# High and low activations as one 512-column operand, summed at the read, and the down products bank by bank, in a float32 transformer stack on one core

## The chip, the cores and the metric

One core of one Trainium2 chip runs the whole kernel. The metric is device time in microseconds, the median of three runs. The engines are named as in the profile: PE is TensorE's matmul stream and PEld its weight loads, DVE is VectorE, ACT is ScalarE, POOL is GpSimd, SP is SyncE, which issues the weights' DMA.

## What is computed

The input is 256 rows of tokens with 1024 features. Five layers follow, all in float32: four of a first block and one of a second.

```python
# first block: layer i has a mixer of kind i % 3 and a feed-forward part
h = layer_norm(ALPHA * h + mix, ln_g[i, 0], ln_b[i, 0])      # retention, rglru, mla, retention
h = layer_norm(ALPHA * h + sq_relu_mlp(h, mlp_w1[i], mlp_w2[i]), ln_g[i, 1], ln_b[i, 1])

def sq_relu_mlp(x, w1, w2):                                   # 1024 -> 4096 -> 1024
    return jnp.square(jax.nn.relu(x @ w1)) @ w2

# second block
x = x + 0.5 * swiglu(rmsnorm(x, ffn1_norm), ffn1_w1, ffn1_w3, ffn1_w2)   # 1024 -> 2816 -> 1024
x = x + hybrid_mixer(rmsnorm(x, mix_norm), ...)               # two attentions with gates
x = x + 0.5 * swiglu(rmsnorm(x, ffn2_norm), ffn2_w1, ffn2_w3, ffn2_w2)
return rmsnorm(x, final_norm)

def swiglu(x, w1, w3, w2):
    return (jax.nn.silu(x @ w1) * (x @ w3)) @ w2
```

## The kernel before

**Split operands.** TensorE takes a float32 operand in one pass only with fewer bits, so each operand is split into a high part (a ScalarE copy to float32r) and a low part (a VectorE subtraction). A product is then three matmuls: high by high, high by low, low by high. `split` does this for activations, `pump` for weights: it issues the DMA of a weight chunk on SyncE up to 8 chunks ahead, and the chunk's cast on ScalarE (line 368, `hl<-raw`) and its low part on VectorE up to 5 chunks ahead. `get` fetches the next chunk and calls `pump`. The transposed activations of a layer are `xT[:, k, a, tok]`: k is one of 8 blocks of 128 features, a is high or low, tok one of 256 tokens, so that `xT[:, k]` is 512 contiguous columns.

**Products.** All matmuls are issued by the helper `mm` at line 315. `ws` holds weights stationary: for each k it issues three matmuls of 256 columns (weights high by x high, weights high by x low, weights low by x high), all into the same 256 columns of a PSUM bank. `xs` holds the activations stationary. `down` is the second product of a feed-forward layer, and the output product of a mixer: hidden values `a` (high) and `b` (low) of one token tile are stationary, and 512 columns of weights move; the six matmuls alternate between the two banks of the tile's accumulators. `down_tail` issues the last chunks of a layer bank by bank. `front` makes the first six chunks of a layer; the two parts of x already go into separate columns there and are summed by `front_sum` when the bank is read: a ScalarE copy to `tmp` (line 549) and a VectorE add.

**PSUM.** Eight banks: four accumulators (`accp`) and a common pool of four (`pp`, taken by `psb`). `front` takes two accumulators and four banks of the pool, the tiles `fr`.

**Order.** The order on every engine is the order of the program text; each engine works its own queue in that order and waits for others by semaphores. In `mlp` a step j makes one chunk of hidden values (two steps share a bank, and the second one reads it: ReLU, square and split on ScalarE and VectorE), and 8 steps later `down` consumes it. `ffn` is alike with two chunks a step and a lag of 5. The recurrent layer `lru` follows the list `LRU_STEPS` from its fourth entry on: "R0 G0 R1 G1 V0 V1 g1 R2 g0 V2 C0 S0 D0 C1 F0 R3 V3 C2 S1 D1 W0 F1 S2 R4 V4 C3 D2 G2 S3 D3 g2 F2 G4 C4 S4 D4 g4 W1 G3 g3 F3 F4 W2 W3 W4". R and G are products with `ws` (two chunks into one bank); V is the convolution on R's bank, first step on ScalarE and six steps on VectorE (`uc`); `gelu_a` reads G's bank with a square on ScalarE and then VectorE; C is the gates' products and ScalarE work, S a square root on ScalarE, D the VectorE chain (`b_`, then `u`) with the scan, F the gated states (`hh`), W the output product. In `mix` the list `MIX_STEPS` does the same for two attentions; it has "Sb0 R1 Nb0 q00 q01 q02 k00 X1 Tb0", where q00 to k00 are products with `ws`, X1 transposes of queries (line 1371) and R1, Nb0 norms on VectorE.

The change touches `ws` (not its body; a sibling is added), `down`, `front_sum`, `mlp`, `ret` (`rope`, `qk`), `lru`, `ffn`, and in `mix` the products of heads of group A (`aproj_qk`) and the gates. In `mla` and in mix's branch products `ws` stays.

Of the kernel before, what the change touches and what calls it, by code (L numbers as in the profile page):

```python
# [9 lines left out]
F32 = mybir.dt.float32  # L10
# [8 lines left out]
P = 128  # L19
S = 256  # L20
# [16 lines left out]
FRONT = 6  # products of a layer that start on the first tile alone  # L37
# chunks at a layer's end that finish the first tile ahead
# [5 lines left out]
MIX_B = (0, 2, 1)  # queries of four heads, keys and values, the other queries  # L44
# R, G, W: products; V: convolution; C, S, D: gates and scan; g: second half of gelu;
# F: the gated states, split
LRU_STEPS = ("R0 G0 R1 G1 V0 V1 g1 R2 g0 V2 C0 S0 D0 C1 F0 R3 V3 C2 S1 D1 W0 F1 S2 R4 "
             "V4 C3 D2 G2 S3 D3 g2 F2 G4 C4 S4 D4 g4 W1 G3 g3 F3 F4 W2 W3 W4").split()
# k, v: keys and values of four heads; q, r, p: queries of two; S, N, T, V: a head's scores,
# norm, transposes and values; o: first rows of the output product  # L50
# [3 lines left out]
# h, j: last chunk of the keys and values, chunks of the last queries of group B; I, R, X:  # L54
# their squares, norm and rope, transposes. q, k, v: projections of a pair of heads of
# group A; S, N, T, V: a head's scores, norm, transposes and values (a: pair, head, tile
# of rows); g: gates; A, B: the branches' products
# [16 lines left out]
def _stream():  # L74
    """Every weight chunk in the order of use: (segment, input, layer, first row,
    row blocks, columns as (start, width) runs)."""
# [126 lines left out]
# chunks that the tensor engine takes whole, as float32  # L203
# [8 lines left out]
# per-partition vectors: name -> (first column, columns)  # L212
# [20 lines left out]
def _consts():  # L233
    """Tables that depend on shapes alone."""
# [47 lines left out]
def kernel(ctx, tc, d, out, dbg=None):  # L282
# [39 lines left out]
    def split(src, h, l):  # L322
        """h + l = src, each of a width that one pass of the tensor engine carries."""
        ns.copy(out=h, in_=src)  # L324
        tt(l, src, h.bitcast(F32), SUB)

# [50 lines left out]
    def low_next(n):  # L377
        """Make the next few of the low parts held back."""
        for _, low in (st["late"] or ())[:n]:
            tt(*low)  # L380
        if st["late"]:
            st["late"] = st["late"][n:]

    def low_parts(late, soon=0):
        """Hold back the low parts of the chunks that come after the next few, or make
        those held back."""
# [8 lines left out]
    def pin(on):  # L395
        """While on, chunks stay until it is off again."""
        st["pin"] = on
        if on:
            st["base"] = st["i"]
# [16 lines left out]
    def ws(ps, ch, xT, kk, c0=0, first=True, last=True):  # L416
        """ps[f, tok] += W[:, c0 + f] . x[tok]; weights stationary."""
# [6 lines left out]

    def xs(ps, ch, xT, t, k0, kk, first, last, w0=0, w=None):
        """ps[tok, n] += x[tok] . W[:, n]; activations stationary."""
# [8 lines left out]
    def xs_front(items, xT, after=None):  # L435
        """Products with stationary activations that begin on the first tile and the
        weights' high parts: yields when the second tile's activations are needed.
        items: name, first block of rows, their number, outs, and if it is the last into
        these; outs[t]: banks, and their columns in the chunk."""
# [21 lines left out]
        if after:  # the first tile ahead  # L461
            order = [(c, t) for t in range(2) for c in range(n)]
# [13 lines left out]
    def down(acc, t, hid, ch, first, last, perm=False):  # L476
        """acc[t][tok, :] += hid[:, tok] . W rows of one block."""
# [6 lines left out]
        for o, w in halves:  # L484
            mm(o, a, l[:, 0, w], False, False)
        for o, w in halves:
            mm(o, b, h[:, 0, w], False, last)

    def down_tail(acc, get_item, n_items, perm=False):
        """The last chunks: the first tile whole, then the second, with two stops before  # L490
        its end. Low parts of the next layer's weights wait till its start."""
# [20 lines left out]
    def front(names, xT, banks, done, stops=(2, 4)):  # L512
        """Products with stationary weights that begin on the first tile alone: yields
        when the second tile's activations are needed. done(n, ps) gets each bank,
        [second][x high, x low][tok], to be summed over the middle."""
# [29 lines left out]
    def front_sum(ps, tmp, o):  # L545
        """o[f, tok] from a bank of front."""
        v = ps.rearrange("p (t a n) -> p t a n", t=2, a=2)
        t3 = tmp.rearrange("p (t n) -> p t n", t=2)
        ns.copy(out=t3, in_=v[:, :, 1])
        tt(o.rearrange("p (t n) -> p t n", t=2), v[:, :, 0], t3, ADD)  # L550

    def front_banks():
        """The first tile's accumulators, then four banks of the common pool."""
# [39 lines left out]
    def rsqrt(o, v, mul, add):  # L593
        """o = (v * mul + add) ** -0.5 for a few columns."""
# [6 lines left out]
    def to_xT(xT, y, t, halves=(0, 1)):  # L601
        for g in halves:
            if t == 0:
                ps = psb("trp")
            else:  # the tile's accumulators are free by then
# [79 lines left out]
    def angles(k):  # L685
        """sin and cos of position times frequency, reduced to within pi of zero."""
# [29 lines left out]
    def gate_tables():  # L716
        # 2 softplus(-lam), and halves of the gate biases
# [30 lines left out]
    def early(j):  # L748
        """Tables of later layers, made in the first layers."""
# [997 lines left out]
```

## Time and profile before

| | |
|---|---|
| median of three runs | 2050.29 us (2049.59 to 2050.74) |
| span of the profiled execution | 2048.1 us |
| PE busy | 2015.0 us, 98% |
| PEld busy | 1814.8 us, 89% |
| DVE busy | 1288.9 us, 63% |
| ACT busy | 1022.5 us, 50% |
| DMA from HBM over the span | 177 GB/s |

The busy time of an engine is the union of its instructions' spans, and matmuls overlap: one of 256 columns is shown with 284 ns from start to end, while the next starts long before. A run of n matmuls that is busy for B and whose matmuls are shown with a latency of L therefore has a rate of (B - L) / (n - 1). In a timeline a row is a run of equal instructions: its start, how long the run was busy, the operation, output and inputs by the program's names, the form of output and input, the count, and in brackets the idle time of the engine before the run and what ended it.

### The profile page before, as it was taken

To read this page: it belongs to the slowest core of one execution; us is meant where nothing else is said; L and a number is where in the kernel's file an instruction comes from. 1 tells how busy PE (TensorE), PEld (TensorE's weight loads), DVE (VectorE), ACT (ScalarE), POOL (GpSimd) and SP (SyncE) were. 2 spreads that over 40 slices of the span, in tenths; PEclk is the share of its full clock that TensorE was granted. 3 is DMA by queue.
4 is the path that set the end of the run, shared out by engine and by line. 5 is a ranking of instruction groups with operands and counts; after the bars stand their busy time and mean duration, and the time that the engine had idled before them with its cause. 6 is when DMAs were issued, how large, how long until landed. Compare 5 with 4: busy or idle time off the path is not lost.

```text
span 2048.1 us, 31960 instructions
## 1 busy us (share of the span) xinstructions
PE 2015.0 (98%) x12814; PEld 1814.8 (89%) x12814; DVE 1288.9 (63%) x1823; ACT 1022.5 (50%) x1493; POOL 72.3 (4%) x114
## 2 busy tenths in 40 slices
PE   8999999999999999999999999999999999999998
PEld 6888989887998889998888899989997999999997
DVE  6667765589645667545766764576557755467554
ACT  5444565485645355554444365544445545445443
POOL 0000000000000100000000100000001100000000
PEclk9999999999999999999999999999999999999999
DMA  8554555464665444654655475546554555365552
GB/s 298 183 174 144 185 197 185 146 209 147 231 199 171 145 133 163 215 188 144 224 176 170 143 279 191 186 144 213 188 176 167 158 139 148 123 201 181 197 186 76
DMA packets 102724, 364.73 MB, mean 178 GB/s; under 512 B 11855, under 2 KB 12527, under 8 KB 102576
## 3 DMA queue, kind: packets, MB, share of 16 engines
q1 hardware_dynamic: 97200, 345.09, 50.3%
q0 software_dynamic: 5376, 17.61, 3.4%
q8 instruction: 100, 1.64, 0.3%
q14 instruction: 48, 0.39, 0.1%
HBM read 360.52 MB, written 2.13 MB: 177 GB/s over the span
## 4 chain that ended last, share of the span: by engine, by line
PE 93%; DVE 4%; ACT 1%; issue 1%; POOL 1%; DMA 0%; SPq 0%; POOLq 0%; ACTq 0%; DVEq 0%
PE pp L315 54%; PE a L315 32%; PE fr L315 4%; DVE x L300 1%; PE ao L315 1%; POOL rs L303 1%; DVE bs L628 1%; DMA raw<-in_w_ret_dram 0%; PE a L609 0%; PE a L1492 0%; ACT hl L368 0%; DVE xT L303 0%; DVE hl L303 0%; PE trp L897 0%; DVE bq L303 0%
## 5 line engine op out<-in xcount | busy, mean ns | idle before, releaser
L303 DVE TENSOR_TENSOR hl<-raw,hl 128x1024 fp32r<-128x1024 f32 (+3 forms) x659 | 765.5, 1200 | 179.9 <-ACT hl L368 179.0
L315 PEld LDWEIGHTS pp<-xT,hl 128*128 128x128 f32 x6384 | 786.8, 192 | 14.4 <-issue 1.6
L315 PE MATMUL pp<-xT,hl 128*128 128x256 f32 x6384 | 798.7, 284 | 0.0
L368 ACT CAST hl<-raw 128x1024 fp32r<-128x1024 f32 (+3 forms) x659 | 650.5, 1031 | 187.7 <-PE a L315 75.7
L315 PE MATMUL a<-hl,h 128*128 128x512 f32 x2064 | 501.8, 394 | 0.0
L315 PEld LDWEIGHTS a<-hl,h 128*128 128x128 f32 x2064 | 381.9, 190 | 75.2
L315 PE MATMUL pp<-hl,xT 128*128 128x512 f32 (+2 forms) x1200 | 269.9, 381 | 2.7 <-ACT hl L368 1.6
L315 PEld LDWEIGHTS pp<-hl,xT 128*128 128x128 f32 x1200 | 219.6, 189 | 40.6 <-DVE xT L303 2.1
L303 DVE TENSOR_TENSOR h<-r,h 128x512 fp32r<-128x512 f32 (+1 forms) x108 | 63.1, 584 | 262.6 <-ACT h L324 262.5
L312 ACT ACTIVATE r<-pp 128x512 f32<-128x512 f32 (+1 forms) x90 | 45.5, 506 | 311.6 <-PE pp L315 311.6
L315 PE MATMUL a<-hl,yT 128*128 128x512 f32 x432 | 104.0, 397 | 0.0
L315 PEld LDWEIGHTS a<-hl,yT 128*128 128x128 f32 x432 | 80.8, 188 | 18.7 <-issue 0.5
L303 POOL TENSOR_TENSOR rs<-ve,mhalf 128x1 f32<-128x1 f32 (+2 forms) x48 | 34.9, 728 | 1745.3 <-DVE ve L306 1741.7
L315 PE MATMUL fr<-xT,hl 128*128 128x256 f32 x672 | 88.4, 285 | 0.0
L324 ACT CAST h<-r 128x512 fp32r<-128x512 f32 (+1 forms) x108 | 57.6, 533 | 57.3 <-DVE r L303 55.2
L315 PEld LDWEIGHTS fr<-xT,hl 128*128 128x128 f32 x672 | 83.4, 192 | 0.0
L300 DVE SCALAR_TENSOR_TENSOR r<-r,pp 128x256 f32<-128x256 f32 x38 | 16.0, 420 | 81.6 <-ACT r L312 81.6
L315 PE MATMUL a<-xT,hl 128*128 128x256 f32 x336 | 45.7, 286 | 4.0 <-DVE xT L303 4.0
L315 PEld LDWEIGHTS a<-xT,hl 128*128 128x128 f32 x336 | 42.1, 191 | 7.5 <-DVE xT L303 7.5
L300 DVE SCALAR_TENSOR_TENSOR x<-x,a 128x512 f32<-128x512 f32 x32 | 21.9, 684 | 32.9 <-PE a L315 32.8
L312 ACT ACTIVATE r<-r 128x512 f32<-128x512 f32 x64 | 40.5, 633 | 2.0
L324 ACT CAST xT<-a 128x512 fp32r<-128x512 f32 x22 | 12.8, 586 | 42.5 <-PE a L609 42.5
(352 smaller groups left out, 1315.1 us busy)
## 6 DMA issues: line engine op xcount, KB each, us to landing
raw<-in_w_mlp_dram SPq DMA_DIRECT2D x256, 512.0 KB, 4.6
raw<-in_w_ffn_dram SPq DMA_DIRECT2D x132, 512.0 KB, 4.5
raw<-in_w_ret_dram SPq DMA_DIRECT2D x128, 512.0 KB, 4.4
raw<-in_w_mix_dram SPq DMA_DIRECT2D x68, 512.0 KB, 4.2
raw<-in_w_lru_dram SPq DMA_DIRECT2D x30, 512.0 KB, 4.7
raw<-in_w_mla_dram SPq DMA_DIRECT2D x12, 512.0 KB, 3.8
raw<-in_w_mix_dram SPq DMA_DIRECT2D x16, 384.0 KB, 3.5
gB<-in_ln_g_dram POOLq DMA_DIRECT2D x8, 512.0 KB, 4.9
```

The lines of the kernel that those rows point to most:

```text
L300: nv.scalar_tensor_tensor(out=o, in0=a, scalar=s, in1=b, op0=op0, op1=op1)
L303: (eng or nv).tensor_tensor(out=o, in0=a, in1=b, op=op)
L312: ns.activation(out=o, in_=i, func=f, **kw)
L315: nt.matmul(out=o, lhsT=a, rhs=b, start=start, stop=stop)
L324: ns.copy(out=h, in_=src)
L368: ns.copy(out=hl[:, 0, :c], in_=t[:, :c])
L628: nv.bn_stats(out=bs[:, n], in_=z[:, w])
```

## The change

A second helper `ws2` is used where `ws` had been with `xT` moving. It issues, for each k, one matmul of 512 columns (weights high by both parts of x, side by side in a whole bank) and one of 256 (weights low by x high, onto the first half). `ws2_sum` adds the halves when the bank is read, with a ScalarE copy and a VectorE add into an SBUF tile, and what read the PSUM bank before reads that tile. Every chunk now takes a bank of its own. `front_sum` copies to its output directly, without `tmp`. `down` issues its six matmuls bank by bank. In `lru` the tag `gs` gets two buffers. The rest of the diff takes comments away and renames ffn's argument.

```diff
+    def ws2(bank, ch, xT, kk, c0=0):
+        h, l = ch
+        w = slice(c0, c0 + P)
+        for k in range(kk):
+            mm(bank, h[:, k, w], xT[:, k], k == 0, False)
+            mm(bank[:, :S], l[:, k, w], xT[:, k, 0, :], False, k == kk - 1)
+
+    def ws2_sum(bank, o):
+        ns.copy(out=o, in_=bank[:, S:])
+        tt(o, bank[:, :S], o, ADD)
...
     def down(acc, t, hid, ch, first, last, perm=False):
...
         for o, w in halves:
             mm(o, a, h[:, 0, w], first, False)
-        for o, w in halves:
             mm(o, a, l[:, 0, w], False, False)
-        for o, w in halves:
             mm(o, b, h[:, 0, w], False, last)
...
-    def front_sum(ps, tmp, o):
+    def front_sum(ps, o):
         v = ps.rearrange("p (t a n) -> p t a n", t=2, a=2)
-        t3 = tmp.rearrange("p (t n) -> p t n", t=2)
-        ns.copy(out=t3, in_=v[:, :, 1])
-        tt(o.rearrange("p (t n) -> p t n", t=2), v[:, :, 0], t3, ADD)
+        o = o.rearrange("p (t n) -> p t n", t=2)
+        ns.copy(out=o, in_=v[:, :, 1])
+        tt(o, v[:, :, 0], o, ADD)
...
                 if j < nf:
                     ch = get("mlp_w1")
+                    ps = psb()
+                    ws2(ps, ch, xT, KD)
                     if j % 2 == 0:
-                        ps = psb().rearrange("p (c n) -> p c n", c=2)
-                    ws(ps[:, j % 2], ch, xT, KD)
+                        su = mp.tile([P, 2, S], F32, tag="su", name="su", bufs=2)
+                    ws2_sum(ps, su[:, j % 2])
                     if j % 2 == 1:
-                        evac(j, ps)
+                        evac(j, su)
...
             def qk(h, nm, mid=None):
-                ps = psb()
+                a = rp.tile([P, 512], F32, tag="ra", name="ra", bufs=1)
+                a = a.rearrange("p (c n) -> p c n", c=2)
                 for c in range(2):
-                    ws(ps[:, c * S:(c + 1) * S], get("ret_w_in"), xT, KD)
+                    ps = psb()
+                    ws2(ps, get("ret_w_in"), xT, KD)
+                    ws2_sum(ps, a[:, c])
                     if c == 0 and mid:
                         mid()
-                hd[h, nm] = rope(ps, nm)
+                hd[h, nm] = rope(a, nm)
...
                 if step in "RG":
-                    ps = psb().rearrange("p (c n) -> p c n", c=2)
+                    tag = "gs" if step == "G" else "xc"
+                    su = lp.tile([P, 2, S], F32, tag=tag, name=tag)
                     for c in range(2):
-                        ws(ps[:, c], get("lru_w_in"), xT, KD)
+                        ps = psb()
+                        ws2(ps, get("lru_w_in"), xT, KD)
+                        ws2_sum(ps, su[:, c])
                     if step == "G":
-                        gelu_a(j, ps)
+                        gelu_a(j, su)
                     else:
-                        xcs[j] = ps
+                        xcs[j] = su
...
                 if j < nf:
-                    ps = psb().rearrange("p (c n) -> p c n", c=2)
-                    ws(ps[:, 0], get(w[0]), xT, KD)
-                    ws(ps[:, 1], get(w[1]), xT, KD)
-                    evac(j, ps[:, 0], ps[:, 1])
+                    su = mp.tile([P, 2, S], F32, tag="su", name="su", bufs=2)
+                    for n in range(2):
+                        ps = psb()
+                        ws2(ps, get(w[n]), xT, KD)
+                        ws2_sum(ps, su[:, n])
+                    evac(j, su[:, 0], su[:, 1])
...
                 ps = psb()
-                ws(ps[:, :S], get("w_in_2"), xT, KD)
-                if c == 0:  # queries of a tile in falling order, as the bias has them
+                ws2(ps, get("w_in_2"), xT, KD)
+                if c == 0:
                     o = qk[:, c, g].rearrange("p (t n) -> p t n", t=2)[:, :, ::-1]
-                    act(o, ps[:, :S].rearrange("p (t n) -> p t n", t=2), AF.Copy, scale=0.125)
+                    v = ps.rearrange("p (a t n) -> p a t n", a=2, t=2)
+                    act(o, v[:, 1], AF.Copy, scale=0.125)
+                    stt(o, v[:, 0], 0.125, o, MUL, ADD)
                 else:
-                    ns.copy(out=qk[:, c, g], in_=ps[:, :S])
+                    ns.copy(out=qk[:, c, g], in_=ps[:, S:])
+                    tt(qk[:, c, g], ps[:, :S], qk[:, c, g], ADD)
...
-                    ws(ps["g"][:, b], get("w_in_2"), xT, KD)
-                    for c in range(2 * b):
-                        act(th[:, 8 * c + n], ps["g"][:, c], AF.Tanh, scale=0.5,
-                            bias=hbg[:, 8 * c + n:8 * c + n + 1])
+                    pg = psb()
+                    ws2(pg, get("w_in_2"), xT, KD)
+                    o = th[:, 8 * b + n]
+                    ws2_sum(pg, o)
+                    act(o, o, AF.Tanh, scale=0.5, bias=hbg[:, 8 * b + n:8 * b + n + 1])
```

## Rows read from the trace of the kernel before

**Rows 1.** Page, part 1: busy time, share of span, instructions.

```profile
PE 2015.0 (98%) x12814; PEld 1814.8 (89%) x12814; DVE 1288.9 (63%) x1823; ACT 1022.5 (50%) x1493; POOL 72.3 (4%) x114
```

**Rows 2.** Timeline of PE, a steady stretch of mlp 0 (columns as told above).

```profile
301.59 3.04 PE L315 MATMUL pp<-xT,hl 128*128 128x256 f32 x24
304.46 2.94 PE L315 MATMUL a<-hl,h 128*128 128x512 f32 x12
307.24 3.04 PE L315 MATMUL pp<-xT,hl 128*128 128x256 f32 x24
```

**Rows 3.** Groups by form, PE: count, busy us, mean ns, idle before.

```profile
L315 PE MATMUL pp<-xT,hl 128*128 128x256 f32 x6384 | 798.7, 284 | 0.0
L315 PE MATMUL pp<-hl,xT 128*128 128x512 f32 x912 | 216.5, 395 | 2.4 <-ACT hl L368 1.6 <-DVE hl L303 0.5 <-DVE xT L303 0.3
```

**Rows 4.** Timeline of PE: values in ret 0; end of mlp 0.

```profile
76.77 11.08 PE L315 MATMUL pp<-hl,xT 128*128 128x512 f32 x48
372.22 23.86 PE L315 MATMUL a<-hl,h 128*128 128x512 f32 x102
```

**Rows 5.** Groups by form, ACT and DVE: the front's sum at the read.

```profile
L549 ACT COPY tmp<-fr 128x256 f32<-128x256 f32 x28 | 9.6, 367 | 0.0
L303 DVE TENSOR_TENSOR su<-fr,tmp 128x256 f32<-128x256 f32 x24 | 9.5, 418 | 0.0
```

**Rows 6.** Timelines of PE and DVE behind the front of mlp 0.

```profile
231.69 8.80 PE L315 MATMUL pp<-xT,hl 128*128 128x256 f32 x72
...
234.53 0.42 DVE L303 TENSOR_TENSOR su<-fr,tmp 128x256 f32<-128x256 f32 x1
...
239.06 0.75 DVE L303 TENSOR_TENSOR su<-fr,tmp 128x256 f32<-128x256 f32 x2
```

**Rows 7.** Timelines of PE and DVE behind the front of ffn 1.

```profile
1372.13 12.04 PE L315 MATMUL pp<-xT,hl 128*128 128x256 f32 x99
...
1375.28 0.42 DVE L303 TENSOR_TENSOR su<-fr,tmp 128x256 f32<-128x256 f32 x1
...
1379.06 0.75 DVE L303 TENSOR_TENSOR su<-fr,tmp 128x256 f32<-128x256 f32 x2
```

**Rows 8.** Timelines of ACT and DVE in lru; last, DVE's group u<-u,e there.

```profile
429.04 1.02 ACT L312 ACTIVATE uc<-pp,vec 128x256 f32<-128x256 f32 x2 [0.26 <-PE pp L315]
443.43 1.01 ACT L312 ACTIVATE uc<-pp,vec 128x256 f32<-128x256 f32 x2
454.28 1.02 ACT L312 ACTIVATE uc<-pp,vec 128x256 f32<-128x256 f32 x2 [1.43 <-PE pp L315]
461.76 0.60 ACT L312 ACTIVATE g<-pp 128x512 f32<-128x512 f32 x1
467.52 0.60 ACT L312 ACTIVATE g<-pp 128x512 f32<-128x512 f32 x1 [0.19 <-PE pp L315]
474.01 0.63 ACT L312 ACTIVATE s__4484<-u 128x512 f32<-128x512 f32 x1
...
432.11 0.69 DVE L300 SCALAR_TENSOR_TENSOR g<-g,gs 128x512 f32<-128x512 f32 x1
444.89 1.26 DVE L300 SCALAR_TENSOR_TENSOR uc<-pp,vec,uc 128x255 f32<-128x255 f32 x3
457.63 2.42 DVE L300 SCALAR_TENSOR_TENSOR uc<-pp,vec,uc 128x255 f32<-128x255 f32 x6
465.99 0.68 DVE L300 SCALAR_TENSOR_TENSOR g<-g,pp 128x512 f32<-128x512 f32 x1
473.93 0.68 DVE L300 SCALAR_TENSOR_TENSOR g<-g,pp 128x512 f32<-128x512 f32 x1
...
L300 DVE SCALAR_TENSOR_TENSOR u<-u,e 128x512 f32<-128x512 f32 x5 | 3.4, 689 | 3.0 <-ACT s__4208 L312 2.6 <-ACT s__4093 L312 0.5
```

**Rows 9.** Timelines of PE and DVE at the start of attention in mix.

```profile
1593.63 1.03 PE L1371 MATMUL trp<-cs,bq 128*128 128x128 f32 x8
...
1593.89 3.82 DVE L303 TENSOR_TENSOR hl<-raw,hl 128x1024 fp32r<-128x1024 f32 x4
```

More of the change, by code (lines that the diff above doesn't have):

```diff
@@ L776, in done @@
                     sums[0] = mp.tile([P, 2, S], F32, tag="su", name="su", bufs=2)
-                tmp = mp.tile([P, S], F32, tag="tmp", name="tmp", bufs=2)
-                front_sum(ps, tmp, sums[0][:, j % 2])
+                front_sum(ps, sums[0][:, j % 2])
                 if j % 2 == 1:
@@ L803, in ret, with rope @@
             hd = {}
-            def rope(ps, nm):
+            def rope(a, nm):
                 cos, sin = trig["cosr"], trig["sinr"]
-                a = rp.tile([P, 512], F32, tag="ra", name="ra", bufs=1)
-                a = a.rearrange("p (c n) -> p c n", c=2)
                 b = rp.tile([P, 2, S], F32, tag="rb", name="rb", bufs=1)
                 o = rp.tile([P, 2, S], F32, tag=nm, name=nm)
-                v = ps.rearrange("p (c n) -> p c n", c=2)
-                tt(a, v, cos[:, None, :].to_broadcast([P, 2, S]), MUL)
-                tt(b, v, sin[:, None, :].to_broadcast([P, 2, S]), MUL)
+                tt(b, a, sin[:, None, :].to_broadcast([P, 2, S]), MUL)
+                tt(a, a, cos[:, None, :].to_broadcast([P, 2, S]), MUL)
                 tt(o[:, 0], a[:, 0], b[:, 1], SUB)
@@ L1023, in finish @@
                 yTs[j] = yT
-            gs = lp.tile([P, 2, S], F32, tag="gs", name="gs", bufs=1)
+            gs = lp.tile([P, 2, S], F32, tag="gs", name="gs")
             def done(n, ps):
@@ L1030, in done @@
                     xcs[j // 2] = lp.tile([P, 2, S], F32, tag="xc", name="xc")
-                tmp = lp.tile([P, S], F32, tag="tmp", name="tmp")
-                front_sum(ps, tmp, gs[:, c] if j == 1 else xcs[j // 2][:, c])
+                front_sum(ps, gs[:, c] if j == 1 else xcs[j // 2][:, c])
                 if c == j == 1:
@@ L1235, in mla, with ffn @@
             yield from down_tail(acc, lambda c: (oT[:, 4 + c], get("mla_w_o")), 4)
-    def ffn(n, xT):
+    def ffn(seg, xT):
         nf = DFF2 // P
         lag = FFN_LAG
-        w = [f"ffn{n}_w{k}_2" for k in (1, 3, 2)]
-        tail = TAIL["ffn", n]
+        w = [f"ffn{seg}_w{k}_2" for k in (1, 3, 2)]
+        tail = TAIL["ffn", seg]
         with tc.tile_pool(name="ffnp", bufs=8) as mp:
@@ L1258, in done @@
                     sums[0] = mp.tile([P, 2, S], F32, tag="su", name="su", bufs=2)
-                tmp = mp.tile([P, S], F32, tag="tmp", name="tmp", bufs=2)
-                front_sum(ps, tmp, sums[0][:, n % 2])
+                front_sum(ps, sums[0][:, n % 2])
                 if n % 2 == 1:
@@ L1264, in ffn @@
             yield from front([w[k % 2] for k in range(FRONT)], xT, front_banks(), done,
-                             (4, 5) if n == 1 else (3, 4))
+                             (4, 5) if seg == 1 else (3, 4))
             acc = acc_new()
@@ L1550, in mix @@
                     b = k[0]
-                    if b == 0:
-                        ps["g"] = psb().rearrange("p (c n) -> p c n", c=2)
-                    ws(ps["g"][:, b], get("w_in_2"), xT, KD)
-                    for c in range(2 * b):
-                        act(th[:, 8 * c + n], ps["g"][:, c], AF.Tanh, scale=0.5,
-                            bias=hbg[:, 8 * c + n:8 * c + n + 1])
+                    pg = psb()
[3 more added lines that the diff above has]
+                    act(o, o, AF.Tanh, scale=0.5, bias=hbg[:, 8 * b + n:8 * b + n + 1])
                 else:
```

## Prediction

> **What bounds the kernel now.** I read the busy line of the page first. TensorE is busy 98% of the span, VectorE 63%, ScalarE 50% [rows 1], so time is made where TensorE's stream gets shorter or where it is made to wait. The second view is the timeline of TensorE in a steady stretch of a feed-forward layer: 24 matmuls of 256 columns, 12 of 512, again 24, with no idle time noted between them, 5.65 us a round [rows 2]. There everything else is hidden. The third view is the timeline of the other two engines in the stretches where they are not hidden: right behind a layer's front, in the middle of the recurrent layer (lru), and at the start of attention in mix. What matters in them is not the busy share but which engine runs behind which, because the change makes ScalarE wait for VectorE in places where today it does not.
>
> The profiled span is 2048.1 us, 2.2 below the median 2050.3; I carry the sum over to the median unchanged.
>
> **The change part by part.**
>
> *One 512-column matmul for two of 256.* In `ws` a step of eight rows of weights issues three matmuls of 256 columns; `ws2` issues one of 512 and one of 256. The columns are the same 768, one matmul and one weight load go. The group that `ws` makes has 6384 matmuls [rows 3], so 2128 steps; by the loops these are 832 in the four mlp, 608 in the two ffn, 256 in the two ret, 320 in mix and 112 in lru, and all of them go over to `ws2`. What is one matmul worth? A run's rate is its busy time less one matmul's latency, over the count less one. 72 matmuls of 256 take 8.80 us [rows 6] with a latency of 0.284 [rows 3], so 119.9 ns each; columns alone at the full 2.4 GHz are 106.7, and 13 ns come on top. For 512 columns the kernel has two rates. Where the transposed activations `xT` are one operand and the split weights `hl` the other, 48 take 11.08 us [rows 4] with a latency of 0.395 [rows 3]: 227.4 ns. Where hidden values are stationary, 102 take 23.86 us: 232.4 ns [rows 4]. The new matmul has the operands of the first row, only with their roles swapped, so I take 227.4. A step then goes from 3 x 119.9 = 359.7 to 227.4 + 119.9 = 347.3: 12.4 ns saved, times 2128 = 26.4 us. The ends: with 232.4 it is 7.4 ns (15.7 us); and the round of [rows 2], 5.65 us, is 16 ns less than 24 x 119.9 + 12 x 232.4 = 5.666, so a change of width may itself give some 8 ns, which would make 20 ns (43 us).
>
> The Trainium skill speaks against this part: TensorE: Matmul & The Clock Gate, section "Back-to-back issue gap", has a fixed cost of only 2.5 ns per matmul beside the columns at 2.4 GHz. The rows above show 13 to 14 ns, so I go by them; by the page's figure the part would be worth 2128 x 2.5 = 5.3 us.
>
> *`down` by bank.* The same twelve matmuls of a pair of tiles in another order. The 102 matmuls in [rows 4] hold both orders: 60 come from `down`, which alternates banks today, and 42 from `down_tail`, which already goes bank by bank. The whole run is at 232.4. I take nothing. Ends: 0, and if it brought 2136 matmuls to 227.4, a gain of 10.7 us. Nothing waits for a bank of `down` alone, since its last flag is never set.
>
> *The sum at the read.* Each of the 266 products of `ws2` adds a ScalarE copy of 256 columns (367 ns) and a VectorE add (418 ns) [rows 5]; two adds in a row take 0.75 [rows 6], so each adds some 0.34 to a full queue. Over the span that is 266 x 0.37 = 98 us of ScalarE and about 90 to 111 us of VectorE, in engines that are idle 1025 and 759 us. In the steady stretch it is free. But both engines work their queues in order, so what counts is where these two stand and who waits behind them. Three places.
>
> *(a) Behind a front.* The front's last four chunks hold all four banks of the common pool. Today two chunks share a bank; now each takes one, so the third chunk behind the front needs the bank of the front's fifth. In mlp 0 the products start at 231.69 [rows 6]. VectorE reads the front's fourth chunk at 234.53 to 234.95 and the fifth and sixth from 239.06 on, the fifth until 239.48. One chunk takes 8 x 347.3 = 2.78: the second chunk is ready to start at 234.47 and waits 0.5; the third is ready at 237.73 and waits 1.75. Together 2.3 us, in all four mlp (the pattern of sums is the same): 9.2. In ffn 1 the products start at 1372.13 and the reads end at 1375.70 and 1379.48 [rows 7]: waits of 0.8 and 1.0, 1.8 us, twice: 3.6. Nothing hides these: TensorE has no other work in its order. The lru front reads early enough.
>
> *(b) The recurrent layer.* Today ScalarE reads a product (convolution, square of the gelu) from PSUM as soon as TensorE is done, and runs ahead of VectorE. From now on the same read needs VectorE's add, and the add stands in VectorE's queue behind older work. How far VectorE trails at each such point is in [rows 8]: start on ScalarE, and start of the VectorE instruction ahead of which the adds will stand: R2 429.04 and 432.11 (3.1 us), R3 443.43 and 444.89 (1.5), R4 454.28 and 457.63 (3.35), G2 461.76 and 465.99 (4.2), G4 467.52 and 473.93 (6.4). Each hold on ScalarE delays the square root that VectorE's next chain needs. The group u<-u,e shows that VectorE waits for exactly these, 0.5 and 2.6 us [rows 8]. Walking it through, with 0.7 for each pair of adds: G1 puts VectorE 1.3 behind (its adds, and ScalarE's square that now starts after them). R2: ScalarE falls back 1.3 + 3.1 + 0.7 = 5.1, and VectorE with it at the first chain. R3: 5.1 + 1.5 + 0.7 = 7.3, passed on again. R4: ScalarE 7.3 + 3.35 + 0.7 = 11.3; VectorE had 2.9 to spare there (457.63 less the end of the first ScalarE step) and falls back to 8.4. G2 leaves VectorE at 8.4 + 0.7 = 9.1. G4: ScalarE 9.1 + 6.4 + 0.7 = 16.2; its square root, 474.01 plus 0.63 today, comes at 490.8, and VectorE's chain, which starts two steps of 0.6 behind 473.93, at 475.1, must wait for it: 15.7. G3 adds 0.7: 16.4. The output product waits for the states of this chain, so the layer ends 16.4 later. Its 112 steps would have gained 1.4, so against the sum above this is a loss of 17.8. Ends: 6.2 if only the work of 14 adds (4.8 us) and the lost 1.4 count, and 25 if every trail adds up (18.6, seven pairs of adds of 0.7, and the 1.4).
>
> *(c) Start of attention in mix.* The four products ahead of the transposes at 1593.63 hold one bank each, and VectorE can free the first only behind the norm of the queries and a weight's low part, which is in its queue from 1593.89 [rows 9]. The four low parts there take 3.82, one of 1024 columns and three of 768, so by columns 1.18 and 0.88. With 0.37 for an add between them the first transposes start at 1593.89 + 1.18 + 0.37 = 1595.4 and the second at 1596.7, against some 1593.7 by TensorE's own pace: 3.0 us. Later the chains of a head have a product of 2.8 us between each two of their steps, and an add of 0.4 more is covered; without that cover it would be up to 0.8 for each of 40 products, 32 us, which I do not expect.
>
> In ret the adds stand ahead of the rope, on VectorE alone, and the products of values run in between (24 matmuls of 512, 5.5 us); nothing is lost there. SyncE's and GpSimd's queues get no instruction more or less; the weights' DMA is asked for by the same calls.
>
> Sum: -26.4 + 9.2 + 3.6 + 17.8 + 3.0 = +7.2 us, so 2057.5.
>
> **The rivals.**
>
> 1. *The lock in lru is cheap* and only the adds' own work counts (6.2 in place of 17.8): 2045.9. For it: VectorE's later chains run without waits today, and a trail that shrinks absorbs the next. Against it: the waits of u<-u,e [rows 8].
> 2. *All copies and adds are covered*, the case on the other side without reserve: -26.4, 2023.9. For it: 98% on TensorE and idle halves elsewhere [rows 1]. It decides if the banks behind a front are free by 237.7 in mlp 0, where [rows 6] says 239.5, and if ScalarE is not held in lru.
> 3. *A change of width pays too*: 20 ns a step, -42.6 + 33.6 = -9: 2041.
> 4. *The 512-column matmul runs at 232.4*: -15.7 + 33 = +17: 2068.
> 5. *A matmul less saves hardly any time*, the columns being all that is paid: then a step gains about 2.5 and the sum is near +28: 2078. The rows of both widths speak against it; this is the page's figure from above.
>
> **How the numbers follow.** My forecast 2057.5 gets 0.50 (own range 2050 to 2064), rival 1 0.20, rival 2 0.10, rival 3 0.06, rival 4 0.10, rival 5 0.04. The range 2040 to 2068 leaves out rival 2, rival 5 and half of rival 4, 0.19. A measurement of this kernel can tell 0.2%, 4.1 us, from no change. Faster by more: rivals 2 and 3 and half of rival 1, 0.26. Within it (2046.2 to 2054.4): half of rival 1 and 0.12 of the forecast, 0.22. Slower: the rest, 0.52.
>
> **What would show it.** Right: steps of 347 ns in the steady stretch, so that a round of an mlp drops from 5.65 to 5.55; two TensorE waits of 0.5 and 1.8 us for VectorE's sums behind each mlp front; in lru waits of ScalarE for VectorE of several us ahead of the convolutions, and a stretch 417 to 489 that becomes about 16 us longer; transposes 3 us later in mix. The tail's 232.4 stays, and `down` with it. Wrong: a round that hardly changes (rival 4 or 5), fronts without waits, or an lru stretch no longer than before (rivals 1, 2).

## The result: 1.3% slower, and the profile after

The changed kernel takes 2076.9 us, the kernel before 2050.4: a ratio of 1.0128 with an interval of 1.0114 to 1.0143. The profiled spans are shorter, 2073.2 and 2048.1 us, a difference of 25.1: a span leaves out some 2 us of each execution, and the execution profiled after was the shortest of its four, 1.8 us under their median. The forecast was a loss of 7.2 us, its range ended at 2068. The sign was right; 19 us of loss were not seen.

The page of the kernel after, part 1 and the engines of the chain that ended last, then that chain in the kernel before:

```profile
PE 2011.8 (97%) x10686; PEld 1704.8 (82%) x10686; DVE 1390.4 (67%) x2089; ACT 1101.3 (53%) x1735; POOL 72.5 (3%) x114
...
PE 79%; DVE 11%; ACT 5%; issue 2%; DMA 1%; POOL 1%; SPq 0%; POOLq 0%; DVEq 0%; ACTq 0%
```

```profile
PE 93%; DVE 4%; ACT 1%; issue 1%; POOL 1%; DMA 0%; SPq 0%; POOLq 0%; ACTq 0%; DVEq 0%
```

Against [rows 1], 2128 matmuls and as many weight loads are gone, but TensorE's busy time fell by only 3.2 us, VectorE got 102 us and ScalarE 79 us more. In the chain TensorE's share is 79%, in the kernel before it is 93%: the end is now set in part by VectorE and ScalarE.

Where the 25.1 us lie, layer by layer (from the first transposition at one border between layers to that at the next, in both traces), beside what the forecast's terms give for each layer:

| layer | before, us | change, forecast | change, measured |
|---|---|---|---|
| ret 0 | 205.7 | -1.6 | +0.2 |
| mlp 0 | 185.6 | -0.3 | +5.6 |
| lru | 102.4 | +16.4 | +18.1 |
| mlp 1, mlp 2, mlp 3 | 183.6, 183.6, 184.9 | -0.3 each | +0.7, +0.7, +1.0 |
| mla | 99.2 | 0 | +0.4 |
| ret 1 | 197.6 | -1.6 | -0.5 |
| ffn 1, ffn 2 | 194.0, 200.7 | -2.0 each | -0.4, -2.1 |
| mix | 306.2 | -1.0 | +1.6 |

So the big place, lru, was seen. Two things were not: nearly every layer gained less than it should have by its matmuls, and mlp 0 lost 5 us that the other mlp did not lose.

**The steady stretch.** Timeline of TensorE in mlp 0 after, the view of [rows 2] (a product's row takes matmuls of 512 and 256 columns together, under the first one's form):

```profile
308.22 2.94 PE L315 MATMUL pp<-xT,hl 128*128 128x512 f32 x16
311.00 2.94 PE L315 MATMUL a<-hl,h 128*128 128x512 f32 x12
313.78 2.97 PE L315 MATMUL pp<-xT,hl 128*128 128x512 f32 x16
...
319.36 2.97 PE L315 MATMUL pp<-xT,hl 128*128 128x512 f32 x16
...
324.95 2.27 PE L315 MATMUL pp<-xT,hl 128*128 128x512 f32 x12
```

Three rounds from 308.22 to 324.95 are 5.58 us each; before it was 5.65, and 5.55 was forecast. Over all products of `ws` and `ws2` in which no matmul starts later than 0.3 us behind the one ahead of it, from their first matmul's start to the start of what follows, a step has a median of 359.1 ns before (169 runs of products) and 351.4 after (134). That is 7.7 ns, not 12.4. By position, as means over 91 such products of mlp and ffn: the first 512-column matmul, which stands behind one of `down`'s 512 columns, takes 228 ns from its start to the next start; the seven others, each behind a 256-column one, 234 to 239; the 256-column ones 115 to 118. I had put in 227.4 and 119.9.

**Behind the fronts.** Timeline of TensorE, then of VectorE, behind the front of mlp 0 (they answer to [rows 6]):

```profile
231.90 2.99 PE L315 MATMUL pp<-xT,hl 128*128 128x512 f32 x16
235.21 3.05 PE L315 MATMUL pp<-xT,hl 128*128 128x512 f32 x16 [0.32 <-DVE su L303]
239.74 3.04 PE L315 MATMUL pp<-xT,hl 128*128 128x512 f32 x16 [1.48 <-DVE su L303]
```

```profile
234.74 0.42 DVE L303 TENSOR_TENSOR su<-fr,su 128x256 f32<-128x256 f32 x1
...
239.27 0.75 DVE L303 TENSOR_TENSOR su<-fr,su 128x256 f32<-128x256 f32 x2
```

The second chunk starts behind VectorE's read of the front's fourth, the third behind that of its fifth. In brackets stand 0.32 and 1.48; from start to start, less the usual spacing, the pauses are some 0.5 and 1.6 us. The forecast said 0.5 and 1.75. The other mlp have the same two waits. In ffn 1 and ffn 2 (the second pair answers for the layer that [rows 7] did not show):

```profile
1402.37 3.08 PE L315 MATMUL pp<-xT,hl 128*128 128x512 f32 x16 [0.92 <-DVE su L303]
1406.15 2.23 PE L315 MATMUL pp<-xT,hl 128*128 128x512 f32 x11 [0.70 <-DVE su L303]
...
1896.04 5.81 PE L315 MATMUL pp<-xT,hl 128*128 128x512 f32 x32
1902.06 4.15 PE L315 MATMUL pp<-xT,hl 128*128 128x512 f32 x22 [0.22 <-DVE su L303]
```

ffn 1 waits 1.6 us, where 1.8 was said; ffn 2 only 0.2. I had carried ffn 1's figure over without reading ffn 2.

**mlp 0 alone.** At step 18 of mlp 0 four small products make the bias tables, each in a bank of the common pool, read by ScalarE (`bv`). No row of them stood in the forecast. Timeline of TensorE before, where they and the product behind them run without a wait; then of TensorE and of ScalarE, after:

```profile
294.01 1.89 PE L315 MATMUL pp<-hot,rb 33*8 33x256 f32 x8
295.83 3.14 PE L315 MATMUL pp<-xT,hl 128*128 128x256 f32 x24
```

```profile
295.75 1.46 PE L315 MATMUL pp<-hot,rb 33*8 33x256 f32 x6
297.98 0.59 PE L315 MATMUL pp<-hot,rb 33*8 33x256 f32 x2 [0.77 <-DVE su L303]
301.16 4.42 PE L315 MATMUL pp<-xT,hl 128*128 128x512 f32 x16 [2.59 <-ACT bv L1306]
```

```profile
297.96 0.63 ACT L312 ACTIVATE r<-su 128x512 f32<-128x512 f32 x1 [1.98 <-DVE su L303]
...
300.75 1.15 ACT L1306 COPY bv<-pp 8x256 f32<-8x256 f32 x4
```

The last small product waits for a bank that VectorE's add holds. ScalarE's copies of the small products stand in its queue behind `r<-su`, which waits for an add too, and behind three more instructions. The next chunk needs one of those banks and starts at 301.16. The product that follows takes 4.42 us in place of 2.94, which the windows explain (columns: busy us and counts of TensorE, its loads, VectorE, ScalarE and GpSimd, then granted clock, DMA share, GB/s):

```profile
296.00:298.00 2.00, 1.23 (x7) 0.34 (x6) 1.93 (x3) 0.04 (x1) 0.00 (x0) 1.00 0.92 342
298.00:300.00 2.00, 0.58 (x2) 0.07 (x2) 0.07 (x1) 1.94 (x4) 0.00 (x0) 1.00 0.96 360
300.00:302.00 2.00, 0.84 (x3) 0.74 (x4) 1.75 (x2) 2.00 (x6) 0.60 (x2) 0.68 0.55 223
302.00:304.00 2.00, 2.00 (x8) 1.71 (x8) 1.22 (x2) 0.85 (x1) 1.41 (x3) 0.50 0.50 96
304.00:306.00 2.00, 2.00 (x12) 1.73 (x12) 0.11 (x1) 0.38 (x2) 0.00 (x0) 0.96 0.77 223
```

TensorE idles for most of 296 to 301, and from then until about 304 the granted clock is 0.50, the 1.2 GHz level: 8 matmuls in the 2 us from 302, where the stretches from 304 to 312 have 11 to 13. In the kernel before, the mean clock of every stretch of mlp 0 and lru is 1.00. The Trainium skill has this in TensorE: Matmul & The Clock Gate, section "What's actually happening": the lower clock is the idle state, and activity lifts it. The rows agree: 0.50 comes behind the idle stretch, and from 304 on, with TensorE busy all the time, the mean is 0.96 again.

**The recurrent layer.** Timeline of ScalarE in lru after: the convolutions' first steps (`uc`), the squares (`g`); then VectorE's last chain and last gated state, then TensorE; last, the rows of the kernel before that answer to those of VectorE and TensorE:

```profile
438.00 0.60 ACT L312 ACTIVATE uc<-xc,vec 128x256 f32<-128x256 f32 x1 [0.16 <-DVE xc L303]
...
468.66 1.09 ACT L312 ACTIVATE uc<-xc,vec 128x256 f32<-128x256 f32 x2 [4.28 <-DVE xc L303]
...
488.52 0.63 ACT L312 ACTIVATE g<-gs 128x512 f32<-128x512 f32 x1 [3.96 <-DVE gs L303]
504.69 0.63 ACT L312 ACTIVATE g<-gs 128x512 f32<-128x512 f32 x1 [4.22 <-DVE gs L303]
```

```profile
495.19 0.69 DVE L300 SCALAR_TENSOR_TENSOR u<-u,e 128x512 f32<-128x512 f32 x1 [3.86 <-ACT s__4194 L312]
...
510.14 0.68 DVE L300 SCALAR_TENSOR_TENSOR hh<-hh,g 128x512 f32<-128x512 f32 x1
```

```profile
468.68 14.16 PE L315 MATMUL pp<-xT,hl 128*128 128x512 f32 x64 [2.98 <-DVE xc L303]
...
509.55 12.85 PE L315 MATMUL a<-hl,yT 128*128 128x512 f32 x42 [5.70 <-ACT yT L324]
```

```profile
475.13 0.69 DVE L300 SCALAR_TENSOR_TENSOR u<-u,e 128x512 f32<-128x512 f32 x1
...
487.91 0.69 DVE L300 SCALAR_TENSOR_TENSOR hh<-hh,g 128x512 f32<-128x512 f32 x1
```

```profile
455.62 11.87 PE L315 MATMUL pp<-xT,hl 128*128 128x256 f32 x96
...
488.13 10.36 PE L315 MATMUL a<-hl,yT 128*128 128x512 f32 x42
```

ScalarE is held by VectorE's adds, and VectorE's chain then waits 3.86 us for ScalarE's square root: the lock, in the places named. The layer starts 5.8 us later than before. Less that, the points of [rows 8] moved like this: R2 by 3.2 (438.00 against 429.04; forecast 5.1), R4 by 8.6 (11.3), G4 by 15.2 (16.2), the last chain's `u<-u,e` by 14.3 (495.19 against 475.13; forecast 15.7). The last gated state, 487.91 in the kernel before, moved by 16.4, which is the forecast's end.

**The start of attention in mix.** Timeline of TensorE, which answers to [rows 9]:

```profile
1621.77 0.66 PE L1386 MATMUL trp<-cs,bq 128*128 128x128 f32 x4 [1.93 <-DVE aqk L300]
1623.10 0.66 PE L1386 MATMUL trp<-cs,bq 128*128 128x128 f32 x4 [0.68 <-ACT qTB L1388]
```

2.9 us of pauses from start to start, where 3.0 was forecast.

### The profile page after: what moved, and what is told of

Its sections match the earlier page's. It is cut to its first block, busy times and chain, and to the rows that moved or that the text cites. A ratio compares the mean times of both kernels' runs of the same rounds, so it can differ in the third digit from the quotient of the medians.

```text
span 2073.2 us, 28098 instructions
## 1 busy us (share of the span) xinstructions
PE 2011.8 (97%) x10686; PEld 1704.8 (82%) x10686; DVE 1390.4 (67%) x2089; ACT 1101.3 (53%) x1735; POOL 72.5 (3%) x114
## 4 chain that ended last, share of the span: by engine, by line
PE 79%; DVE 11%; ACT 5%; issue 2%; DMA 1%; POOL 1%; SPq 0%; POOLq 0%; DVEq 0%; ACTq 0%
PE pp L315 46%; PE a L315 29%; DVE hl L303 4%; ACT hl L368 2%; PE fr L315 2%; DVE x L300 1%; ACT r L312 1%; DVE su L303 1%; POOL rs L303 1%; PE ao L315 1%; DVE bs L639 1%; DVE bq L303 0%; ACT h L324 0%; DMA raw<-in_w_ret_dram 0%; PE a L620 0%
## 5 line engine op out<-in xcount | busy, mean ns | idle before, releaser
L315 PE MATMUL pp<-xT,hl 128*128 128x512 f32 (+1 forms) x4256 | 788.2, 341 | 14.7 <-DVE su L303 8.9
L315 PEld LDWEIGHTS pp<-xT,hl 128*128 128x128 f32 x4256 | 663.9, 189 | 122.1 <-DVE su L303 12.5
L368 ACT CAST hl<-raw 128x1024 fp32r<-128x1024 f32 (+3 forms) x659 | 658.0, 1034 | 130.8 <-PE a L315 72.5
L435 ACT COPY su<-pp 128x256 f32<-128x256 f32 x180 | 67.1, 373 | 245.0 <-PE pp L315 245.0
L303 DVE TENSOR_TENSOR su<-pp,su 128x256 f32<-128x256 f32 x180 | 75.9, 422 | 119.0 <-ACT su L435 118.9
L312 ACT ACTIVATE r<-su 128x512 f32<-128x512 f32 (+1 forms) x108 | 59.0, 546 | 73.3 <-DVE su L303 72.5
```

The lines of the kernel that those rows point to most:

```text
L303: (eng or nv).tensor_tensor(out=o, in0=a, in1=b, op=op)
L312: ns.activation(out=o, in_=i, func=f, **kw)
L315: nt.matmul(out=o, lhsT=a, rhs=b, start=start, stop=stop)
L368: ns.copy(out=hl[:, 0, :c], in_=t[:, :c])
L435: ns.copy(out=o, in_=bank[:, S:])
```

## The experiments

After these readings the theory was: the mechanisms are as forecast, and what was missed is the price of a step and mlp 0's bias tables. Rivals: the price of 12.4 ns stands and the sums cost more than seen; or a matmul less is worth only 2.5 ns.

**What the width is worth, on the changed kernel.**

```diff
-            mm(bank, h[:, k, w], xT[:, k], k == 0, False)
+            mm(bank[:, :S], h[:, k, w], xT[:, k, 0, :], k == 0, False)
+            mm(bank[:, S:], h[:, k, w], xT[:, k, 1, :], False, False)
             mm(bank[:, :S], l[:, k, w], xT[:, k, 0, :], False, k == kk - 1)
```

> The changed kernel with its 512-column matmul taken apart again into two of 256 columns, each half of the bank its own; sums, banks and waits stay as they are. It isolates what the width is worth. Theory A (read from both traces: three of 256 take 3 x 120.2 = 360.6 ns, one of 512 and one of 256 take 234.3 + 117.4 = 351.7): 8.9 ns a step, 19 us slower than the changed kernel, 2096. Rival B, the price of the forecast (12.4 ns): 26 us slower, 2103, and then something else than the width must have eaten what was missed. Rival C (2.5 ns, the figure of the Trainium skill's page TensorE: Matmul & The Clock Gate, section Back-to-back issue gap): 5 us slower, 2082.

Measured: 2087.1 us (ratio to before 1.0176, 1.0162 to 1.0190), 10.2 more than the changed kernel. Less than theory A, more than C. The median of undisturbed products is again 359.1 ns a step, so the rate is as in the kernel before; but a slower TensorE waits less for the other two engines (in the two traces, 8.2 us for the sums `su` in place of 9.7). mlp 1 grows by 1.5 us (7.0 ns for each of its 208 steps). lru is 1.6 shorter, which tells nothing of the width: two runs below that leave lru alone have it as short, at 118.9 and 119.1 us. This kernel mixes the price with the waits and can't settle it; the last two runs below do.

**The order within a product.**

```diff
         for k in range(kk):
             mm(bank, h[:, k, w], xT[:, k], k == 0, False)
+        for k in range(kk):
             mm(bank[:, :S], l[:, k, w], xT[:, k, 0, :], False, k == kk - 1)
```

> The changed kernel with the order within a product turned: first its eight matmuls of 512 columns, then its eight of 256. Nothing else. Theory A1: the 234 ns of the 512-column matmul come from the alternation with 256 columns; in a run it goes at the 227 of the rows that I took, and a step costs 227.4 + 119.9 = 347.3, 4.4 less than now: 9 us faster than the changed kernel, 2068. Theory A2: the rate belongs to this matmul with activations moving, whatever stands beside it: 2077, within 2 us. Rival: the change of width itself gives time, as the rows of before seemed to say (16 ns per 36 matmuls): slower, by up to 2128 x 5 = 10 us, 2087.

Measured: 2072.1 us (1.0103, 1.0090 to 1.0117), 4.8 less than the changed kernel, half of what A1 said. The rates are those of A1: by position over 91 products, all eight 512-column matmuls take 227 ns (226.5 to 227.5), the first 256-column one, behind a wide one, 113, the others 120, and an undisturbed product takes a median of 346.4 ns a step. mlp 1 to 3 gain 1.1 us each; mix loses 1.5 us and ffn 1 loses 0.6. In mix TensorE idles only 0.3 us longer, but behind its wait at the transposes the mean granted clock is 0.59 over 4 us where it is 1.00 in the changed kernel, and at the start of ffn 1 it is 0.60 over 4 us; at mlp 0's bias tables the waits grow by 0.4 and the product behind them by 0.8. So the lower clock took back some of what the grouping gave. The two durations taken in the forecast were thus right for runs and wrong for the order in which the change puts them.

**`down` alone.** The kernel before with the six matmuls of `down` bank by bank, as in the diff.

> The kernel before with the new order of the down products alone. Theory: no gain, 2050, at most 1 us slower, as the 231.5 to 232.0 ns of these matmuls in the two traces say. Rival: the order brings them to 227.4 and saves up to 10.7 us (2040), and the changed kernel lost as much elsewhere.

Measured: 2049.8 us (0.9998, 0.9989 to 1.0006). Nothing, as the forecast took.

**The recurrent layer as before.** In the branch for R and G, the lines of the kernel before stand again:

```diff
-                    su = lp.tile([P, 2, S], F32, tag=tag, name=tag)
+                    ps = psb().rearrange("p (c n) -> p c n", c=2)
                     for c in range(2):
-                        ps = psb()
-                        ws2(ps, get("lru_w_in"), xT, KD)
-                        ws2_sum(ps, su[:, c])
+                        ws(ps[:, c], get("lru_w_in"), xT, KD)
...
```

> The changed kernel with the R and G products of the recurrent layer as before (three matmuls of 256, ScalarE and VectorE read the bank itself). Theory: the layer's 18.0 us go back, 2059. Rival: the lock there is not what costs, the layers' borders or the rates shift the loss elsewhere: 2070 or more. If the wider matmul's gain of 1 us on its 112 steps were all that counts: 2078.

Measured: 2058.1 us (1.0035, 1.0022 to 1.0048), 18.8 less than the changed kernel; the layer takes 103.1 us, before 102.4 and after 120.5. By the traces 17.4 of it lie in the layer itself, so its loss comes with this edit and does not turn up elsewhere.

**The hold or the work.** Is it that ScalarE stands behind the add, or the 14 copies and adds themselves? `yard` is a tile of zeros and `dum` is read by nobody; the kernel leaves out the term by x low in these products.

```diff
...
                         ws2(ps, get("lru_w_in"), xT, KD)
-                        ws2_sum(ps, su[:, c])
+                        ns.copy(out=su[:, c], in_=ps[:, :S])
+                        tt(dum, ps[:, S:], yard, ADD)
```

> The changed kernel; in the recurrent layer ScalarE copies the first half of each R and G bank to where the sum had gone, and VectorE adds the second half to a spare tile that nobody reads. Same matmuls, same copies, same adds in the same places, but what follows on ScalarE no longer waits for VectorE's add; the term x low is left out of these products. Theory, the hold (ScalarE behind an add that stands in VectorE's queue): only the work of 14 adds stays (4.8 us by the forecast), the layer falls from 120.5 to about 107 us, the whole to 2064. Rival, the work itself (14 copies and 14 adds more in two queues that feed each other): no change, 2077.

Measured: 2063.3 us (1.0066, 1.0049 to 1.0083), 13.6 less than the changed kernel; the layer takes 108.8 us. TensorE in lru of this kernel, the rows that answer to 468.68 and 509.55 above:

```profile
466.79 11.57 PE L315 MATMUL pp<-xT,hl 128*128 128x512 f32 x64 [1.88 <-ACT th L312]
500.19 10.86 PE L315 MATMUL a<-hl,yT 128*128 128x512 f32 x42 [0.83 <-ACT yT L324]
```

The two long waits shrink from 2.98 and 5.70 to 1.88 and 0.83, and the clock falls no more (64 matmuls in 11.57 us in place of 14.16; the granted clock is 1.00 over the whole layer). So 11.7 of 18.1 us are the hold with what the clock adds. The 6.4 us that stay over the kernel before answer to the 4.8 that the forecast had named for the work of the 14 adds (its 6.2 counts 1.4 of lost gain on top, which is no part of the layer's growth).

**The bias tables.**

```diff
-        elif j == 18:
+        elif j == 34:
             bias_vectors()
```

> The changed kernel with the four small products of the bias tables (their matmuls, ScalarE copies and four banks) moved from step 18 of mlp 0 to step 34, where no new products are made any more. Theory: the 4.0 us of waits around them in mlp 0 go, and with them the stretch of about 3.4 us behind them that ran at half the clock (1.7 us): mlp 0 falls from 191.2 to about 185.7, the whole by 5.5 to 2071. Rival: the waits belong to the sums of mlp 0, whose VectorE is late there anyhow, and only move: 2075 or more.

Measured: 2067.5 us (1.0087, 1.0072 to 1.0102), 9.4 less than the changed kernel. mlp 0 falls from 191.2 to 186.3 us, 4.9, near the 5.5 expected. The rest isn't the bias tables': by layers 1.6 of it lies in lru, which takes 118.9 us here and 119.1 in the next run, where mlp 0 keeps its tables; and the traces differ by 1.9 less than the medians, since that of the changed kernel is of its shortest execution.

**The fronts.** The first two chunks of mlp and ffn behind a front as before, in one bank; mlp's lines, those of ffn are alike:

```diff
+                    if j < FRONT + 2:
+                        if j % 2 == 0:
+                            su = psb().rearrange("p (c n) -> p c n", c=2)
+                        ws(su[:, j % 2], ch, xT, KD)
+                    else:
...
```

> The changed kernel with the first two products behind each front of the mlp and ffn layers as before: two chunks in one bank, by three matmuls of 256. Theory: the bank waits behind the fronts (0.45 and 1.64 us in four mlp, 1.08 and 0.86 in ffn 1, 0.38 in ffn 2, 10.7 together) go, less 0.9 for 96 steps at the old width: 9.8 us less, 2067. Rival: VectorE has to read the front's banks all the same and TensorE meets the next bank late: 2073 or more.

Measured: 2064.0 us (1.0069, 1.0054 to 1.0084), 12.9 less than the changed kernel. All four mlp gain 2.1 to 2.2 us, ffn 1 0.8 and ffn 2 0.4, together 9.6 against 9.8 expected. Another 1.4 is in lru, which this edit doesn't touch. The windows around the 2.98 us wait of lru, first in the changed kernel, then in this one, show what differs:

```profile
465.50:468.50 3.00, 0.19 (x1) 0.00 (x0) 3.00 (x4) 0.00 (x0) 0.00 (x0) 0.91 0.31 53
468.50:471.50 3.00, 2.82 (x9) 2.44 (x10) 2.65 (x8) 2.81 (x5) 0.00 (x0) 0.50 0.73 294
471.50:474.50 3.00, 3.00 (x11) 2.52 (x11) 2.96 (x6) 3.00 (x8) 0.00 (x0) 0.50 0.01 3
```

```profile
463.00:466.00 3.00, 0.18 (x1) 0.00 (x0) 3.00 (x4) 0.00 (x0) 0.00 (x0) 1.00 0.30 104
466.00:469.00 3.00, 2.83 (x9) 2.45 (x10) 2.65 (x8) 2.82 (x5) 0.00 (x0) 0.56 0.74 244
469.00:472.00 3.00, 3.00 (x16) 2.57 (x16) 2.96 (x6) 3.00 (x8) 0.00 (x0) 0.87 0.00 1
```

The same wait, the same work behind it, but the clock falls earlier and stays at its lower level for longer in the first: the 64 matmuls behind the wait take 14.16 us there and 12.95 here.

**All of it together.** The changed kernel with the passes grouped, lru as before, the bias tables at step 34, the fronts' next two chunks and the first four products of mix's attention with `ws`.

> All that came out together: the changed kernel with the passes of a product grouped (eight of 512, then eight of 256), the recurrent layer as before, the bias tables at step 34, the first two products behind each front and the first four of mix's attention in the old way. 1888 steps then go from 360.6 to 347.3 ns: 25.1 us. Theory: 2025 if all covers hold, 2030 with some 5 us of small waits left in ret, mix and ffn. Rival: the waits only move (VectorE busy 67% instead of 63%): 2040 or more.

Measured: 2030.2 us, a ratio of 0.9905 (0.9890 to 0.9920): 1% faster than the kernel before and 2.2% faster than the changed one. Page, part 1, and three products of the steady stretch of mlp 0:

```profile
PE 1993.5 (98%) x10926; PEld 1715.2 (85%) x10926; DVE 1377.6 (68%) x2059; ACT 1092.5 (54%) x1709; POOL 72.4 (4%) x114
```

```profile
302.61 2.93 PE L315 MATMUL pp<-xT,hl 128*128 128x512 f32 x16
...
308.15 2.93 PE L315 MATMUL pp<-xT,hl 128*128 128x512 f32 x16
...
313.69 2.93 PE L315 MATMUL pp<-xT,hl 128*128 128x512 f32 x16
```

A round takes 5.54 us. mlp 1 is 2.5 us shorter than before, which is 192 steps at 13.2 ns. mix saves only 2.1 on 288 steps, where 3.8 would be due; TensorE idles 0.6 us more there, and the rest is open.

**The order and the width without the waits.** The combined kernel, first with the passes alternating as in the change, then also with two matmuls of 256 for one of 512.

> The combined kernel without the grouping of the passes: 512 and 256 columns alternate again, as in the changed kernel. With the three waits gone nothing else should hide or give back what a step costs. Theory: 351.7 instead of 347.3 ns on 1888 steps, 8.3 us slower than the combined kernel, 2038.5. Rival: grouping was worth 4.8 us where it was tried on the changed kernel, so the rates in the trace overstate it: 2035 or less.

> The combined kernel with each 512-column matmul taken apart into two of 256 (three matmuls a step, as before the change, sums and banks as in the combined kernel). Theory: 360.6 ns a step, 13.3 more than the combined kernel on 1888 steps, 25.1 us: 2055, which is 5 us over the kernel before, the rest of the small waits in ret, mix and ffn. Rival: the undoing of the width gave 10.2 us where 19 were to be had, so a step in this form costs less than the 360.6 of the kernel before, or the width is worth only half: 2042.

Measured: 2037.0 us (0.9936, 0.9922 to 0.9949) and 2050.9 us (1.0002, 0.9993 to 1.0010). So in 1888 steps the alternation costs 6.8 us, 3.6 ns a step over all, and 5.8 in mlp 1 (1.1 us on 192 steps); the whole width with grouped passes is worth 20.7 us, 11.0 ns a step over all and 13.3 in mlp 1 (2.5 us on 192). Both are under the expected 8.3 and 25.1, as ret and mix don't pass all of it on. Between these two kernels themselves lies the price of the form that the change gave its products, with the waits gone: 13.9 us, 7.4 ns a step, beside the 7.7 of the rates and the 12.4 of the forecast. By the 2.5 ns of the Trainium skill (TensorE: Matmul & The Clock Gate, section "Back-to-back issue gap") an estimate for the width is 4.7 us here; the run shows over four times that. The section gives its 2.5 ns for a single matmul by itself and says that in a stream of weight loads and matmuls, which this is, both set the spacing. The profile's page for the last of these kernels, part 1:

```profile
PE 2014.3 (98%) x12814; PEld 1813.5 (89%) x12814; DVE 1378.7 (67%) x2059; ACT 1093.0 (53%) x1709; POOL 72.5 (4%) x114
```

TensorE does what it did in the kernel before [rows 1], VectorE 90 and ScalarE 71 us more, and the time is the same. Away from the four places (lru, the bias tables, the fronts, the start of mix's attention), the sum at the read is free, to within some 2 us.

## Why the prediction was right and wrong

**The failed step: the price of a step.** It took two durations, 227.4 and 119.9 ns, each from a run of equal matmuls [rows 4, 6], and used them for a sequence in which the two alternate. In a run they hold (227 and 120 in the grouped kernel, 346.4 ns a step); in alternation every wide matmul that follows a narrow one takes 7 to 12 ns more, the narrow ones only 2 to 5 less, and a step takes 351.4. So the term was 7.7 ns by the rates and 7.4 by the last two kernels, instead of 12.4; by the rates the 2016 steps outside lru gained 9.5 us less than was put down, over half of the miss. Rival 4 had this size, but for another reason (a flat 232.4). Rival 3, that a change of width pays, had it the wrong way round: with fewer changes of width the kernel was 4.8 and 6.8 us faster.

**The second failed step, a wait put at nothing: mlp 0's bias tables.** The forecast looked for places where banks of the pool run short behind a front, in lru and in mix, and not at the small products that the hook puts into mlp 0's steps. It cost 4.9 us, of which the half clock behind it is a part.

**The lock in lru was right, in place and in size:** 16.4 forecast, 18.1 measured. The walk's inner steps were 1 to 3 us too large and the last one too small (G3 was given 0.7; ScalarE waits there 4.22 for the add). The waits of TensorE that it makes pull the clock down, which the forecast had not priced; the lru of two other runs with the same program there, 118.9 and 119.1 us, say that some 1.5 us of the 18.1 vary from execution to execution, with the clock. The run without the hold puts 6.4 on the work and 11.7 on the hold with its clock; the forecast's walk had 4.8 and 11.6.

**The fronts and mix's start were right:** 2.3 us forecast and 2.1 measured in each mlp, 1.8 and 1.6 in ffn 1, 3.0 and 2.9 in mix. ffn 2 was 0.2 instead of 1.8: a figure carried over to a layer that was not read.

**`down` and the sums elsewhere were right:** nothing, each shown by a run of its own.

Of the 17.9 us between forecast and measured spans, the steps make 9.5, the bias tables 4.9, lru 1.7, ffn 2 gives 1.4 back. Some 3 us stay open, by layers 1.2 in ret 0, 0.5 in ret 1, about 1 in mix and 0.4 in mla beyond what the steps explain; no run separates them, and mla, the same program in the changed kernel and in four of the runs, took 98.7 to 100.1 us there.

Rival 5 met the time (2078) by a mechanism that is not there. Its matmul gain of 5.3 us is refuted by the runs on width; the number came out near by luck, because the gain that was there was eaten by alternation and by waits that nobody had counted. A time that fits doesn't confirm its story.

## What to carry to other kernels

A rate read from a run of equal matmuls holds for such a run: if an edit makes two widths alternate, order the loop so that each width runs by itself, or price the alternation. When a read of PSUM becomes a sum on two engines, the matmuls are not where to look: look for each place where one engine ran ahead of the other or where every bank was taken, small side products among them, and leave the old form there. The edit that lost 1.3% everywhere gains 1% where it is kept out of four places and its loop is turned.

## What the runs showed of the hardware

A 512-column matmul behind a 256-column one takes 234 to 239 ns, behind another of 512 columns 226 to 228; a 256-column one behind a wide one takes 113 to 118 in place of 120. Alternating is so the dearer order: 351.4 ns a pair against 346.4 sorted by width, with the same weights, operands and banks. Why, no run here tells.

The granted clock fell to 0.50 behind TensorE's waits of 2.98 and 5.70 us in lru and behind the idle stretch of mlp 0, not behind the waits of 1.88 and 0.83 us in lru without the hold; and the price is not fixed: the same wait of 2.98 us was followed by 14.16 us for 64 matmuls in one execution and by 12.95 in another.
